# A decoder layer in split products: the bias table's exchange and the sums of the spatial weights multiplied with rounded and rest halves in place of plain f32 operands

## The chip, the cores and the metric

One NeuronCore of a Trainium2 chip runs the whole layer. The metric is the device time of one execution in microseconds (us); lower is better. TensorE multiplies, VectorE, ScalarE and GpSimd do the rest of the arithmetic, SyncE (SP) issues most of the transfers between DRAM and the on-chip memory. Each engine works through its own instructions in order and waits on semaphores of the others.

## The reference

A hybrid decoder layer over 2048 tokens of width 1024. What the change touches is the relative-position bias of the windowed attention, and the row sums of the spatial weights of the gated group.

```python
def chunked_spatial_gating(u, v, v_g, v_b, w_s, b_s):
    vg = v.reshape(b, s, A_GROUPS, A_GROUP_W)
    vg = (vg - mu) * lax.rsqrt(var + EPS)              # mu, var over the last axis
    vg = vg * v_g + v_b
    w = w_s * causal[None]                             # 4 x 128 x 128
    sv = jnp.einsum('gts,bnsgc->bntgc', w, vc) + b_s.T[None, None, :, :, None]
    return u * sv.reshape(b, s, A_WIDTH)

def sliding_window_attention(q, k, v, sinks, rel_bias):
    ...
    dist = qi + CHUNK - kj                             # 128 queries, 256 keys
    bias = rel_bias.astype(jnp.float32)[t5_causal_buckets(dist)]
    logits = jnp.where(valid, logits + bias, NEG)
    ...

def reference(...):
    h = rms_norm(x, pre_norm_g)
    a_u, a_v, sq, sk, sv, mq, z = jnp.split(h @ w_in, split_at, axis=-1)
    y_a = chunked_spatial_gating(gelu(a_u), gelu(a_v), ...)
    y_b = sliding_window_attention(sq, sk, sv, attn_sinks, rel_bias)
    y_c = memory_cross_attention(mq, *jnp.split(rms_norm(mem) @ w_mem_kv, 2))
    y = jnp.concatenate([y_a, y_b, y_c], axis=-1) * silu(z)
    return x + rms_norm(y @ w_out, post_norm_g)
```

## The kernel before, in words

The tokens are worked in four tiles (t = 0 to 3) of 512. For each tile the input projection is done unit by unit: four units of v, then sv, k, q_0, q_1, mq_0, mq_1, and the units of z and u, with the attention and gating work of the tile between them. The output projection follows. All numbers are f32, and large products are done in split form: an operand X is held as a rounded half (type float32r, made by a ScalarE copy) and the rest (X minus the rounded half, made by VectorE or GpSimd, also float32r). The helper `split(hi, lo, src)` makes both, and products add rounded x rounded, rounded x rest and rest x rounded in one PSUM bank. A few small products use plain f32 operands. TensorE works each plain f32 product as two recorded instructions.

TensorE's and SP's instructions run in the order of the code. VectorE, ScalarE and GpSimd are ordered by a scheduler when the program is built.

Weights come as units of 128x1024: `wraw` (raw, loaded by SP, three buffers), then `whl` (both halves), with the rest half on GpSimd for units 4 to 16 of the order and on VectorE else. In tile 0 there is also work that is done once:
- `first_stats` loads tile 0's rows of x (`xp`, four blocks in two buffers), ScalarE squares and sums them, VectorE (`rsa_x`) and GpSimd (`rsr_x`) make the row factors 1/rms. Everything that leaves PSUM in tile 0 is multiplied by these: v by ScalarE (`sc_v`), sv and k by VectorE (`sc_sv`, `sc_k`) with `bcs`, the factors spread along a row by a small product (`bc`).
- `load_constants` loads the spatial weights (`wsp`), their bias, and the sinks (`sink_bc`); GpSimd clears the triangle of `wsp`.
- `bias_vector` (in the first v unit) multiplies the bias table by a one-hot pattern into 4 x 383 numbers (`bv`), ScalarE copies them to `bvs` and issues their store to DRAM (`vec_d`). `bias_rows` (in the second v unit) is an SP load that reads this vector back with overlapping rows: 128 partitions, each with four runs of 256 numbers, every partition one number further on. `bias_turned` turns the order of the partitions by a product with an anti-diagonal matrix (`turn`), in two banks (`bt`), and ScalarE copies them to `bias`.
- `bias_constants` sums the columns of `wsp` by a product with a matrix of ones (`ad`), and VectorE makes `addend` of it. `bias_constants` and `bias_turned` stand on TensorE behind group q_0.

PSUM has two pools of four banks: `ps_mm` for groups and `ps_t` for the rest (among them g_sv, bc, g_k of tile 0, svt, ad, and both bt, which take the four banks in turn). A bank is free when VectorE or ScalarE has read the tile in it: `bt_1` stands where g_k stood, which `sc_k` reads.

`svt` are four transposes of `sc_sv`, in the middle of group g_q_0. The VectorE work of that stretch of tile 0 is the gelu and the normalization of v (`e_v`, `G_v`, `bn_stats`, `rsa_v`), the memory tokens (`hT<-mt`), `sc_sv` and `sc_k`. The order of SP's loads there is wraw_5, xp (third block), bias_rows, wraw_6, xp (fourth block), wraw_7, wsp, and so on.

Of the kernel before, what the change touches and what calls it, by code (L numbers as in the profile page):

```python
# [9 lines left out]
F32 = mybir.dt.float32  # L10
F32R = mybir.dt.float32r
# [38 lines left out]
def kernel(  # L50
# [33 lines left out]
    def f32(ap):  # L84
        return ap.bitcast(F32)
# [4 lines left out]
    def split(hi, lo, src, lo_engine=None, urgent=False):  # L90
        a = nc.scalar.copy(hi, src)  # L91
        b = (lo_engine or nc.vector).tensor_tensor(lo, src, f32(hi), ALU.subtract)  # L92
        if urgent:
            given["scalar"], given["vector"] = a, b
# [101 lines left out]
    ident = cp.tile([P, P], F32, name="ident")  # L196
    make_identity(nc, ident)

    turn = cp.tile([P, P], F32, name="turn")
    nc.gpsimd.memset(turn, 0.0)  # L200
    nc.gpsimd.affine_select(turn, turn, [[1, P]], ALU.not_equal, 1.0, base=1 - P, channel_multiplier=1)
    mhalf = tiny.tile([P, 4], F32, tag="mhalf", name="mhalf", bufs=1)
    nc.vector.memset(mhalf, -0.5)
    colt = tiny.tile([P, 24], F32, tag="colt", name="colt", bufs=1)
# [130 lines left out]
    wsp = cp.tile([P, 4, P], F32, name="wsp")  # L335
    bsp_t = sp.tile([P, 512], F32, tag="xk", name="bsp_t", bufs=2)
    sink_bc = tiny.tile([P, 4], F32, tag="sink_bc", name="sink_bc", bufs=1)
    ones = cp.tile([P, P], F32, name="ones")
    addend = cp.tile([P, 4, P], F32, name="addend")
    g_v = tiny.tile([P, 4], F32, tag="g_v", name="g_v", bufs=1)  # L340
    bias = cp.tile([P, 4, 256], F32, name="bias")
    vec_d = dram.tile([4, 383], F32, name="vec_d")

    def load_constants():
        nc.sync.dma_start(wsp, wspT)
        nc.sync.dma_start(bsp_t, bsp.broadcast_to([P, 512]))
        nc.sync.dma_start(sink_bc, sinks.broadcast_to([P, 4]))
        nc.vector.memset(ones, 1.0)
        nc.vector.tensor_scalar(g_v, colt[:, 16:20], 0.25, None, ALU.mult)

        nc.gpsimd.affine_select(wsp, wsp, [[0, 4], [1, P]], ALU.is_ge, 0.0, base=0, channel_multiplier=-1)

    def bias_constants():

        ad = ps_t.tile([P, 4, P], F32, tag="t", name="ad")
        nc.tensor.matmul(ad, ones, wsp, start=True, stop=True)
        for g in range(4):
            nc.vector.scalar_tensor_tensor(addend[:, g, :], ad[:, g, :], colt[:, 20 + g : 21 + g],
                                           bsp_t[:, g * P : (g + 1) * P], ALU.mult, ALU.add)
        nc.vector.tensor_scalar(addend, addend, 0.25, None, ALU.mult)  # L360

    def bias_vector():

        bv = ps_t.tile([4, 383], F32, tag="t", name="bv")
        nc.tensor.matmul(bv, rel_t, hot_t, start=True, stop=True)
        bvs = sp.tile([4, 383], F32, tag="e", name="bvs", bufs=3)
        nc.scalar.copy(bvs, bv)
        nc.scalar.dma_start(vec_d, bvs)

    def bias_rows():  # L370

        src = bass.AP(tensor=vec_d.tensor, offset=vec_d.offset, ap=[[1, P], [383, 4], [1, 256]])
        late["rows"] = sp.tile([P, 4, 256], F32, tag="O", name="bias_rows", bufs=1)
        nc.sync.dma_start(late["rows"], src)

    def bias_turned():

        for i in range(2):
            hs = slice(2 * i, 2 * i + 2)
            bt = ps_t.tile([P, 2, 256], F32, tag="t", name=f"bt_{i}")  # L380
            nc.tensor.matmul(bt, turn, late["rows"][:, hs, :], start=True, stop=True)
            nc.scalar.copy(bias[:, hs, :], bt)


# [309 lines left out]
    for t in range(NT):  # L694
# [14 lines left out]
        def run_jobs(first, last):  # L709

            for s in range(first, last):
                for job in jobs.pop(s, []):
                    job()
            tick[0] += 4
            flush_stores()
# [85 lines left out]
            nc.scalar.copy(KK[64:128, kv, :, P:], f32(KK[0:64, kv, :, P:]))  # L801

        run_jobs(-8, -4)

        def values(i):
            if i == (2 if t == 0 else 0):
# [450 lines left out]
```

## Time and profile before

| what | value |
|---|---|
| median of 3 runs | 765.74 us (765.73 to 765.94) |
| the profiled execution | 764.75 us, of it 762.9 us span of the engines |
| TensorE busy | 753.4 us, 99% of the span |
| VectorE, ScalarE, GpSimd busy | 565.9, 398.1, 113.0 us |
| DRAM traffic | 193.98 MB, mean 254 GB/s |

The span is the time between the first and the last instruction that the profiler saw, the execution's own time lies 1.85 us above it. A busy share is an average over the stages; a line of the timeline gives start, duration, engine, source line, operation and operands, and in brackets how long the engine sat idle before and what ended that.

### The profile page before, as it was taken

How to read it: one execution, taken by the hardware profiler on the slowest of the kernel's cores; microseconds unless marked ns; L12 is line 12 of the kernel's file. 1: busy time of each engine (PE TensorE's matmuls, PEld its weight loads, DVE VectorE, ACT ScalarE, POOL GpSimd, SP SyncE). 2: the span in 40 equal slices, each digit the busy share in tenths (PEclk: the TensorE clock that was granted, in tenths of full speed). 3: DMA queues.
4: the chain of work that ended last, by engine and by line, in shares of the span. 5: the costliest groups of instructions: out<-in, count | busy, mean ns of one | idle time of the engine just before them, and what ended most of it. 6: DMA issues, size and time to landing. Idle time of an engine off the chain costs nothing.

```text
span 762.9 us, 10628 instructions
## 1 busy us (share of the span) xinstructions
PE 753.4 (99%) x3764; PEld 636.3 (83%) x3764; DVE 565.9 (74%) x1072; ACT 398.1 (52%) x881; POOL 113.0 (15%) x122
## 2 busy tenths in 40 slices
PE   9999999999999999999999999999999999999995
PEld 7878988888888888888888888888888888888884
DVE  6396899996568888753889789748976325985787
ACT  7686775654735654455465454554444234443441
POOL 0556231000203200011132000201300000120002
PEclk9999999999999999999999999999999999999999
DMA  8847388977477898827779978664574699937618
GB/s 333 302 167 275 127 295 277 323 292 277 162 258 276 310 318 297 297 74 277 223 274 300 344 271 295 209 233 162 161 243 146 224 390 398 369 119 267 248 39 321
DMA packets 54134, 193.98 MB, mean 254 GB/s; under 512 B 5532, under 2 KB 6081, under 8 KB 44865
## 3 DMA queue, kind: packets, MB, share of 16 engines
q1 hardware_dynamic: 53552, 192.70, 71.4%
q8 instruction: 30, 0.49, 0.3%
q10 hardware_dynamic: 528, 0.59, 0.2%
q14 instruction: 24, 0.19, 0.1%
HBM read 140.84 MB, written 52.44 MB: 253 GB/s over the span
## 4 chain that ended last, share of the span: by engine, by line
PE 99%; DVE 0%; issue 0%; DVEq 0%; POOL 0%; ACT 0%; ACTq 0%; POOLq 0%
PE g_z L321 23%; PE g_u L321 12%; PE v L744 12%; PE g_q L321 6%; PE g_mq L321 6%; PE X_S L1108 6%; PE Y_S L1108 6%; PE Y L1108 6%; PE g_k L321 3%; PE X L1108 3%; PE g_sv L321 3%; PE o_c L572 2%; PE l_b L497 2%; PE l_c L548 2%; PE o_b L532 2%; PE sg L883 2%
## 5 line engine op out<-in xcount | busy, mean ns | idle before, releaser
L321 PE MATMUL g_z<-hT,whl 128*128 128x512 f32 x768 | 193.7, 396 | 0.0
L321 PEld LDWEIGHTS g_z<-hT,whl 128*128 128x128 f32 x768 | 138.4, 188 | 25.0
L321 PE MATMUL g_u<-hT,whl 128*128 128x512 f32 x384 | 97.7, 396 | 0.0
L744 PE MATMUL v<-whl,hT 128*128 128x512 f32 x384 | 88.5, 390 | 0.0
L744 PEld LDWEIGHTS v<-whl,hT 128*128 128x128 f32 x384 | 71.7, 188 | 15.8 <-issue 0.6
L321 PEld LDWEIGHTS g_u<-hT,whl 128*128 128x128 f32 x384 | 69.2, 188 | 12.7
L91 ACT CAST whl<-wraw 128x1024 fp32r<-128x1024 f32 (+1 forms) x43 | 44.2, 1027 | 35.2 <-DMA wraw<-in_wst 12.8
L191 POOL TENSOR_TENSOR rsr_v<-rsa_v,mhalf 128x4 f32<-128x4 f32 x16 | 16.8, 1055 | 213.0 <-DVE mv L769 193.2
L92 DVE TENSOR_TENSOR whl<-wraw,whl 128x1024 fp32r<-128x1024 f32 (+1 forms) x30 | 35.8, 1197 | 14.3 <-ACT whl L91 14.2
L321 PE MATMUL g_q<-hT,whl 128*128 128x512 f32 x192 | 45.9, 394 | 0.0
L321 PE MATMUL g_mq<-hT,whl 128*128 128x512 f32 x192 | 44.7, 389 | 0.0
L1108 PE MATMUL Y_S<-hT,yop_S 128*128 128x512 f32 x192 | 44.2, 389 | 0.0
L1108 PE MATMUL Y<-hT,yop 128*128 128x512 f32 x192 | 43.8, 389 | 0.0
L522 POOL TENSOR_SCALAR_AFFINE_SELECT pp_b<-po_b 128x512 fp32r<-128x512 f32 x30 | 20.6, 688 | 148.1 <-ACT po_b L91 148.1
L1108 PEld LDWEIGHTS Y<-hT,yop 128*128 128x128 f32 x192 | 36.0, 188 | 7.5
L1108 PEld LDWEIGHTS Y_S<-hT,yop_S 128*128 128x128 f32 x192 | 36.0, 188 | 7.5
L321 PEld LDWEIGHTS g_q<-hT,whl 128*128 128x128 f32 x192 | 35.8, 188 | 7.8 <-ACT SV L91 0.2
L321 PEld LDWEIGHTS g_mq<-hT,whl 128*128 128x128 f32 x192 | 35.8, 188 | 7.3
L1013 POOL TENSOR_TENSOR r<-a,mhalf 128x1 f32<-128x1 f32 x16 | 13.6, 853 | 190.9 <-DVE a L1011 184.8
L92 POOL TENSOR_TENSOR whl<-wraw,whl 128x1024 fp32r<-128x1024 f32 x13 | 31.6, 2439 | 30.7 <-ACT whl L91 30.2
L558 ACT ACTIVATE L_c<-l_c,nm_c 128x256 f32<-128x256 f32 x48 | 22.3, 471 | 24.5 <-DVE nm_c L553 24.3
L984 DVE TENSOR_TENSOR yop<-y,yop 128x1024 fp32r<-128x1024 f32 x12 | 14.6, 1219 | 24.0 <-ACT yop L975 24.0
(213 smaller groups left out, 1467.4 us busy)
## 6 DMA issues: line engine op xcount, KB each, us to landing
whl<-split_d SPq DMA_DIRECT2D x50, 1024.0 KB, 6.4
wraw<-in_wst SPq DMA_DIRECT2D x41, 512.0 KB, 5.9
split_d<-whl SPq DMA_DIRECT2D x18, 1024.0 KB, 8.0
hT<-wo_B SPq DMA_DIRECT2D x10, 1024.0 KB, 8.9
wo_T<-hT SPq DMA_DIRECT2D x8, 1024.0 KB, 8.5
xr<-in_x SPq DMA_DIRECT2D x16, 512.0 KB, 7.5
y<-yd SPq DMA_DIRECT2D x7, 1024.0 KB, 10.6
xj<-in_xT SPq DMA_DIRECT2D x12, 512.0 KB, 7.7
```

The costliest lines, as they stand in the source:

```text
L91: a = nc.scalar.copy(hi, src)
L92: b = (lo_engine or nc.vector).tensor_tensor(lo, src, f32(hi), ALU.subtract)
L191: nc.gpsimd.tensor_tensor(r, a, mhalf[:, :c], ALU.pow)
L321: nc.tensor.matmul(ps, w[:, wi, k * P : (k + 1) * P], hT[:, hi, k, :], start=(n == 0), stop=(n == 3 * KC - 1))
L497: nc.tensor.matmul(lg[:, e, :], S[kv][:, e, c * P : (c + 1) * P], KK[:, kv, s, c * P : c * P + 256], start=(s == 0), stop=(s == 1))
L522: nc.gpsimd.affine_select(prev[:, s], f32(own[:, s]), [[0, 4], [-1, P]], ALU.is_gt, 0.0, base=0, channel_multiplier=1)
L532: nc.tensor.matmul(o[:, kv, :], SV[:, c + w, kv].rearrange("p a b -> p (a b)"), pT, start=(n == 0), stop=(n == len(terms) - 1))
L548: nc.tensor.matmul(lg[:, e, :], S[:, h % 2, q0 : q0 + P], MK[:, h, s, :], start=(s == 0), stop=(s == 1))
L558: last = nc.scalar.activation(p[:, e, :], lg[:, e, :], AF.Exp, bias=nm[:, e : e + 1], scale=scale, accum_out=den[:, e : e + 1])
L572: nc.tensor.matmul(o, MV[:, j, h].rearrange("p a b -> p (a b)"), pT[:, s, j, :], start=(n == 0), stop=(n == 3))
L744: nc.tensor.matmul(vps[i], hT[:, hi, 2 * j + kk, i * P : (i + 1) * P], w[:, wi, kk * 512 : (kk + 1) * 512], start=(j == 0 and (hi, wi, kk) ...
L1108: nc.tensor.matmul(banks[m], a(s, k)[:, m * P : (m + 1) * P], w(v, k), start=first and n == 0, stop=n == 11, skip_group_check=not first)
```

## The change

`ones`, `turn`, `wsp`'s copy for the column sums and the bias vector become float32r operands. `ones` and `turn` hold numbers that need no rest. `bvs` gets two halves, both are stored to DRAM by one transfer (`vec_d` is [4, 2, 383] now) and read back by two SP loads in place of one, into buffers with the tags "O" and "S1" ("S1" held the second pair of x^T blocks before). `split_spatial`, behind the k unit of tile 0, splits `wsp`; the products of the gating (L883) keep the plain `wsp`. `ad` and the two `bt` become two float32r products each, rounded half and rest into the same bank.

```diff
-    turn = cp.tile([P, P], F32, name="turn")
-    nc.gpsimd.memset(turn, 0.0)
-    nc.gpsimd.affine_select(turn, turn, [[1, P]], ALU.not_equal, 1.0, base=1 - P, channel_multiplier=1)
+    turn = cp.tile([P, P], F32R, name="turn")
+    turn_0 = sp.tile([P, P], F32, tag="ZB", name="turn_0", bufs=2)
+    nc.gpsimd.memset(turn_0, 0.0)
+    nc.gpsimd.affine_select(turn, turn_0, [[1, P]], ALU.not_equal, 1.0, base=1 - P, channel_multiplier=1)
...
-    ones = cp.tile([P, P], F32, name="ones")
+    ones = cp.tile([P, P], F32R, name="ones")
...
-    vec_d = dram.tile([4, 383], F32, name="vec_d")
+    vec_d = dram.tile([4, 2, 383], F32, name="vec_d")
...
-        nc.vector.memset(ones, 1.0)
+        ones_1 = sp.tile([P, P], F32, tag="ZB", name="ones_1", bufs=2)
+        nc.vector.memset(ones_1, 1.0)
+        nc.vector.tensor_copy(ones, ones_1)
...
-        nc.tensor.matmul(ad, ones, wsp, start=True, stop=True)
+        for i, part in enumerate(late["wsp"]):
+            nc.tensor.matmul(ad, ones, part, start=i == 0, stop=i == 1)
...
-        bvs = sp.tile([4, 383], F32, tag="e", name="bvs", bufs=3)
-        nc.scalar.copy(bvs, bv)
-        nc.scalar.dma_start(vec_d, bvs)
+        bvs = sp.tile([4, 2, 383], F32R, tag="pT", name="bvs")
+        split(bvs[:, 0], bvs[:, 1], bv)
+        nc.scalar.dma_start(vec_d, f32(bvs))
...
-        src = bass.AP(tensor=vec_d.tensor, offset=vec_d.offset, ap=[[1, P], [383, 4], [1, 256]])
-        late["rows"] = sp.tile([P, 4, 256], F32, tag="O", name="bias_rows", bufs=1)
-        nc.sync.dma_start(late["rows"], src)
+        late["rows"] = [sp.tile([P, 4, 256], F32R, tag=tag, name=f"bias_rows_{tag}", bufs=1) for tag in ("O", "S1")]
+        for i, rows in enumerate(late["rows"]):
+            src = bass.AP(tensor=vec_d.tensor, offset=vec_d.offset + 383 * i, ap=[[1, P], [766, 4], [1, 256]])
+            nc.sync.dma_start(f32(rows), src)
+
+    def split_spatial():
+        late["wsp"] = [sp.tile([P, 4, P], F32R, tag="ZB", name=f"wsp_{i}", bufs=2) for i in range(2)]
+        split(*late["wsp"], wsp)
...
-            nc.tensor.matmul(bt, turn, late["rows"][:, hs, :], start=True, stop=True)
+            for n, rows in enumerate(late["rows"]):
+                nc.tensor.matmul(bt, turn, rows[:, hs, :], start=n == 0, stop=n == 1)
...
         run_jobs(-8, -4)
+        if t == 0:
+            split_spatial()
```

Three places show how instructions stand now. The first is SP's queue in the second v unit of tile 0, the kernel before and then the changed one (numbers at the end of a name count tiles and differ between the two).

```order
L138 DMA wraw_5_219<-in_wst 128x1024
L225 DMA xp_221<-in_x 128x1024
L374 DMA bias_rows<-vec_d 128x4x256
L138 DMA wraw_6_257<-in_wst 128x1024
L225 DMA xp_221<-in_x 128x1024
L138 DMA wraw_7_296<-in_wst 128x1024
```

```order
L138 DMA wraw_5_221<-in_wst 128x1024
L226 DMA xp_223<-in_x 128x1024
L379 DMA bias_rows_O<-vec_d 128x4x256
L379 DMA bias_rows_S_251<-vec_d 128x4x256
L138 DMA wraw_6_261<-in_wst 128x1024
L226 DMA xp_223<-in_x 128x1024
L138 DMA wraw_7_300<-in_wst 128x1024
```

A second load of rows stands ahead of wraw_6 and of the fourth block of x. The second place is VectorE in tile 0 between the row factors' first step (`rsa_x`) and `bcs`, before and then changed.

```order
L189 TENSOR_SCALAR rsa_x_261<-ss_156 128x4
L491 COPY Lc_b_0_743<-sink_bc 128x4
L790 TENSOR_SCALAR rstd_q<-rsr_x_263 128x4
L491 COPY Lc_b_1_817<-sink_bc 128x4
L583 SCALAR_TENSOR_TENSOR e_v_0_346<-e_v_0_346,sc_v_344 128x512
L583 SCALAR_TENSOR_TENSOR e_v_1_374<-e_v_1_374,sc_v_372 128x512
L407 SCALAR_TENSOR_TENSOR hT_92<-mt_328,colt,hT_92 128x256 x4
L583 SCALAR_TENSOR_TENSOR e_v_2_402<-e_v_2_402,sc_v_400 128x512
L277 COPY bcs_495<-bc_490 128x512
```

```order
L189 TENSOR_SCALAR rsa_x_265<-ss_157 128x4
L501 COPY Lc_b_0_756<-sink_bc 128x4
L800 TENSOR_SCALAR rstd_q<-rsr_x_267 128x4
L501 COPY Lc_b_1_830<-sink_bc 128x4
L92 TENSOR_TENSOR wsp_546<-wsp,wsp_545 128x512
L593 SCALAR_TENSOR_TENSOR e_v_0_352<-e_v_0_352,sc_v_350 128x512
L593 SCALAR_TENSOR_TENSOR e_v_1_380<-e_v_1_380,sc_v_378 128x512
L278 COPY bcs_501<-bc_496 128x512
L417 SCALAR_TENSOR_TENSOR hT_92<-mt_334,colt,hT_92 128x256 x4
```

The subtraction for `wsp`'s rest stands ahead of `e_v_0`, and `bcs` has moved ahead of the memory tokens' `hT`. (On ScalarE the copy for `wsp`'s rounded half stands behind the three `sc_v` and ahead of `e_v_0`; in the first v units VectorE has `bvs`' subtraction just ahead of `whl_3`, and ScalarE issues `vec_d` behind `whl_3`'s copy and ahead of `hT`, as before.) The third place is VectorE a little later, from `sc_sv` on, before and then changed.

```order
L330 TENSOR_TENSOR sc_sv_499<-g_sv_465,bcs_495 128x512
L769 BN_AGGR mv_0_353<-st_0_352 128x2 x2
L769 BN_AGGR mv_1_381<-st_1_380 128x2 x4
L189 TENSOR_SCALAR rsa_v_0_362<-mv_0_353 128x4
L189 TENSOR_SCALAR rsa_v_1_390<-mv_1_381 128x4
L583 SCALAR_TENSOR_TENSOR e_v_3_430<-e_v_3_430,sc_v_428 128x512
L330 TENSOR_TENSOR sc_k_531<-g_k_506,bcs_495 128x512
```

```order
L331 TENSOR_TENSOR sc_sv_505<-g_sv_471,bcs_501 128x512
L779 BN_AGGR mv_0_359<-st_0_358 128x2 x2
L779 BN_AGGR mv_1_387<-st_1_386 128x2 x4
L189 TENSOR_SCALAR rsa_v_0_368<-mv_0_359 128x4
L189 TENSOR_SCALAR rsa_v_1_396<-mv_1_387 128x4
L331 TENSOR_TENSOR sc_k_537<-g_k_512,bcs_501 128x512
L593 SCALAR_TENSOR_TENSOR e_v_3_436<-e_v_3_436,sc_v_434 128x512
```

`sc_k` has moved ahead of `e_v_3`. GpSimd's order in this stretch (`whl_6`, `rsr_x`, `wsp`, `whl_7`, `rsr_mem`, `whl_8`) is as before.

## Rows read from the trace of the kernel before

**Rows 1.** The page of the profile, its span, TensorE's line of part 1 (busy us, share of the span, instructions), the clock line of part 2 (tenths of full speed in 40 slices) and the first line of part 4 (the chain that ended last, by engine).

```profile
span 762.9 us, 10628 instructions
PE 753.4 (99%) x3764; PEld 636.3 (83%) x3764; DVE 565.9 (74%) x1072; ACT 398.1 (52%) x881; POOL 113.0 (15%) x122
...
PEclk9999999999999999999999999999999999999999
...
PE 99%; DVE 0%; issue 0%; DVEq 0%; POOL 0%; ACT 0%; ACTq 0%; POOLq 0%
```

**Rows 2.** The list of waits of TensorE over the whole span (us in total, times, longest).

```profile
PE warm L213 <- POOL ident masks.py:199: 1.5, 1, 1.5
```

**Rows 3.** The timeline of TensorE's products from 34 to 70 us (start us, us from first start to last end, engine, line, operation, out<-in, count).

```profile
34.52 5.72 PE L321 MATMUL g_k<-hT,whl 128*128 128x512 f32 x24
40.08 4.25 PE L321 MATMUL g_q<-hT,whl 128*128 128x512 f32 x18
44.16 0.60 PE L809 MATMUL svt<-ident,sc_sv 128*128 128x128 f32 x4
44.52 1.64 PE L321 MATMUL g_q<-hT,whl 128*128 128x512 f32 x6
45.99 1.02 PE L356 MATMUL ad<-wsp,ones 128*128 128x512 f32 x2
46.85 1.88 PE L381 MATMUL bt<-bias_rows,turn 128*128 128x512 f32 x4
...
54.03 11.04 PE L321 MATMUL g_mq<-hT,whl 128*128 128x512 f32 x48
64.91 4.24 PE L321 MATMUL g_z<-hT,whl 128*128 128x512 f32 x18
```

**Rows 4.** The timeline of TensorE's loads of weights from 43 to 49 us, same columns; in brackets the idle time before and what ended it.

```profile
43.93 0.58 PEld L809 LDWEIGHTS svt<-ident,sc_sv 128*128 128x128 f32 x4
...
47.50 0.40 PEld L381 LDWEIGHTS bt<-bias_rows,turn 128*128 128x128 f32 x2 [0.46 <-DVE sc_k L330]
...
48.56 5.20 PEld L321 LDWEIGHTS g_q<-hT,whl 128*128 128x128 f32 x23 [0.24 <-issue]
```

**Rows 5.** The timeline of ScalarE and of its DMA queue (ACTq) from 13 to 35 us.

```profile
13.87 1.04 ACT L91 CAST whl<-wraw 128x1024 fp32r<-128x1024 f32 x1
14.00 0.26 ACTq L368 DMA_DIRECT2D vec_d<-bvs  x1
14.90 1.34 ACT L288 ACTIVATE hT<-xj,colt 128x512 fp32r<-128x512 f32 x2
...
26.74 1.05 ACT L91 CAST whl<-wraw 128x1024 fp32r<-128x1024 f32 x1 [2.75 <-DMA wraw<-in_wst]
...
31.43 1.84 ACT L762 ACTIVATE sc_v<-v,rsr_x 128x512 f32<-128x512 f32 x3 [1.09 <-POOL rsr_x L191]
33.16 1.16 ACT L582 ACTIVATE e_v<-sc_v 128x512 f32<-128x512 f32 x2
```

**Rows 6.** The timeline of SP, which issues nearly all loads and stores, from 18 to 22 us (here the us are those that the issue takes).

```profile
18.64 0.33 SPq L225 DMA_DIRECT2D xp<-in_x  x1
19.06 1.86 SPq L374 DMA_DIRECT2D bias_rows<-vec_d  x1
21.02 0.46 SPq L138 DMA_DIRECT2D wraw<-in_wst  x1
```

**Rows 7.** The DMA view of three stretches: SP's queue from 18.5 to 21.5 us (packets, MB, share of the 16 engines' time), all packets and SP's queue from 21.5 to 24.5 us, and all packets from 25 to 28 us.

```profile
q1 hardware_dynamic: 183, 0.64, 64.2%
...
DMA packets 563, 0.66 MB, mean 220 GB/s; under 512 B 21, under 2 KB 529, under 8 KB 563
...
q1 hardware_dynamic: 563, 0.66, 92.6%
...
DMA packets 336, 1.21 MB, mean 404 GB/s; under 512 B 37, under 2 KB 37, under 8 KB 336
```

**Rows 8.** The timeline of GpSimd from 30 to 47 us.

```profile
30.38 1.02 POOL L191 TENSOR_TENSOR rsr_x<-rsa_x,mhalf 128x4 f32<-128x4 f32 x1
...
31.98 2.39 POOL L92 TENSOR_TENSOR whl<-wraw,whl 128x1024 fp32r<-128x1024 f32 x1
...
43.75 2.40 POOL L92 TENSOR_TENSOR whl<-wraw,whl 128x1024 fp32r<-128x1024 f32 x1
```

**Rows 9.** The timeline of VectorE from 13 to 48 us.

```profile
13.15 1.41 DVE L289 SCALAR_TENSOR_TENSOR hT<-xj,colt,hT 128x512 fp32r<-128x512 f32 x2
...
32.65 1.75 DVE L491 COPY Lc_b<-sink_bc 128x4 f32<-128x4 f32 x1 [2.35 <-DMA sink_bc<-in_sinks]
...
34.38 0.16 DVE L491 COPY Lc_b<-sink_bc 128x4 f32<-128x4 f32 x1
34.45 1.28 DVE L583 SCALAR_TENSOR_TENSOR e_v<-e_v,sc_v 128x512 f32<-128x512 f32 x2
...
43.01 0.65 DVE L330 TENSOR_TENSOR sc_sv<-g_sv,bcs 128x512 f32<-128x512 f32 x1
...
44.00 2.18 DVE L189 TENSOR_SCALAR rsa_v<-mv 128x4 f32<-128x4 f32 x1
46.17 0.68 DVE L583 SCALAR_TENSOR_TENSOR e_v<-e_v,sc_v 128x512 f32<-128x512 f32 x1
46.77 0.68 DVE L330 TENSOR_TENSOR sc_k<-g_k,bcs 128x512 f32<-128x512 f32 x1
```

## The prediction

> **What bounds the kernel now.** I read the page first. TensorE is busy for 753.4 of 762.9 us, the chain that ended last is TensorE for 99%, and the granted clock stands at full speed in every slice [rows 1]. The list of who TensorE waited for has one entry, 1.5 us at the very start [rows 2]. So the kernel is a line of products without gaps. A microsecond taken out of that line is a microsecond of the result, and so is every wait put into it, because nothing later has slack to swallow it.
>
> Then I read the timeline of the stretch that the change touches, 13 to 50 us. On TensorE [rows 3] the eye should follow svt, ad and bt in the middle of the groups g_q. A rounded 128x512 product takes 10.88 / 48 = 0.227 us (g_mq, 54.03 to 64.91). A plain one is two records of 0.43: ad from 45.99 to 46.85. The loads of weights [rows 4] show what the modelled ends hide: bt's second product had to wait for sc_k on VectorE until 47.50 (sc_k frees the PSUM bank of g_k, which bt_1 takes), and group g_q_1 runs at its pace from 48.56 on. The other place is svt: VectorE ended sc_sv at 43.01 + 0.65 = 43.66, and TensorE came for it at 43.93, so there is only 0.27 us of slack [rows 4, 9].
>
> What feeds these two places? Going back: sc_sv is the end of a VectorE run without a gap that begins at 34.45 (e_v_0) and lasts 9.21 us. It begins when one tiny copy (Lc_b<-sink_bc) lets go at 32.65 + 1.75 = 34.40, a copy that takes 1.75 us, where the next of its kind takes 0.16, because GpSimd's whl_7 runs until 31.98 + 2.39 = 34.37 [rows 8, 9]. GpSimd got there after rsr_x, which needs the fourth block of x (xp), and that block lands behind wraw_6. ScalarE shows it: it waits 2.75 us for wraw_6 until 26.74 [rows 5]. And wraw_6 stands on SP's queue just behind bias_rows, whose issue alone takes 1.86 us [rows 6]. **So the load of bias_rows stands at the head of a tight chain: bias_rows, wraw_6, xp, rsr_x, whl_7, VectorE's run, sc_sv, TensorE.**
>
> **What the change does to it, part by part.**
>
> *The products.* ad and two bt: 3 x 0.86 = 2.58 us go, six rounded ones of 0.227 = 1.36 come. At most 1.2 us is won, if TensorE never waits there.
>
> *The rest of the bias vector.* VectorE computes bvs' second half. It is free at 13.15 + 1.41 = 14.56 [rows 9]; a 128x512 subtraction from PSUM takes 0.65 (sc_sv), so 383 columns take 0.49 and end at 15.05, before whl_3's rounded half is there (13.87 + 1.04 = 14.91, so VectorE loses 0.1). But ScalarE's DMA issue of vec_d now waits for it, 15.05 in place of 14.00, and with its 0.26 holds the next instruction, hT, to 15.3 instead of 14.90 [rows 5]. ScalarE has no gap between there and the xp squares, so SP's next load, xp at 18.64, which waits for these squares, slips by 0.4. Where vec_d's later write would still be on its way when bias_rows is issued (19.5 in place of 19.06), that adds up to 0.5; no row tells when it landed, only that it was before 19.06.
>
> *The second load of rows.* This is the part that costs. SP issues a second 512 KB load of 1 KB pieces: 1.9 us more before wraw_6. So by the issue alone wraw_6 is late by 0.4 + 1.9 = 2.3. By the DMA engines it is more: from 21.5 to 24.5 they moved 508 packets of about 1 KB (0.52 MB) and 0.14 MB of others at a busy share of 92.6%; the others take 0.14 / 0.404 = 0.35 us, the 1 KB packets therefore 0.926 x 3.0 - 0.35 = 2.4 us [rows 7]. Then wraw_6 is late by 0.4 + 2.4 = 2.8. I take 2.6 and call it d. The lower bound is 1.7, if 512 KB took only 0.52 / 0.404 = 1.3 us as loads of large packets do; the upper is 3.3 with vec_d's 0.5. The page "DMA: Bandwidth & Descriptors" of the Trainium skill (section Specifications) speaks for that lower bound: line rate from 512 B on. By that rule d is 1.7; the trace's 1 KB packets at about 220 GB/s do not bear it out.
>
> *Down the chain with d = 2.6.* rsr_x ends at 31.40 + 2.6 = 34.0 (TensorE reaches bc before that and waits 0.3 to 0.5, which is not added: it waits longer at svt anyway). whl_7 ends at 34.37 + 2.6 = 36.97, and the held copy with it.
>
> *The split of the spatial weights.* Its rounded half is a ScalarE CAST of 512 columns, taken as one of the three sc_v, (33.16 - 31.43) / 3 = 0.58 [rows 5], put behind them: 33.16 + 2.6 + 0.58 = 36.34, in time for VectorE's subtraction at 37.05. That subtraction (0.60, as e_v from start to start: 1.28 for two of 0.68) [rows 9] is new in front of e_v_0, so the run starts at 34.45 + 2.6 + 0.6 = 37.65 and ends 9.21 later: sc_sv at 46.86. ScalarE is 3.2 late there too, but its results (e_v's tanh) are still wanted later than they come. Without that cover the CAST would cost 0.58 more.
>
> *TensorE.* svt starts 0.25 after sc_sv: 47.1 in place of 44.16. From svt to ad it is 1.83, so ad at 48.93, bt_0 at 49.4, bt_1 ready at 49.85. Now sc_k: VectorE's rsa_v before it was held by GpSimd's whl_8 (44.00 to 46.18 against 43.75 + 2.40 = 46.15) [rows 8, 9]. whl_8 follows a small GpSimd operation (rsr_mem) whose input comes out of the same VectorE run, some 3.0 later, so it runs to 49.2; sc_k now stands ahead of e_v_3 and gains that 0.6: 49.25 to 49.95. bt_1 starts at 50.2 and its two products end at 50.65. Before, that point was 48.6. **The sum: 2.0 us later**, with the 1.2 of the shorter products already in it. If rsa_v slips in ahead of whl_8, bt_1 goes at 49.85 and the delay is 1.75. Small sets (memsets, the CAST of ones, turn through a second tile) run before 2 us on idle engines, and cost nothing; later groups find their weights halves ready several us ahead (g_mq at 56 wants whl_8, done at 49.2), so nothing is added there.
>
> The profiled execution has a span of 762.9 and a time of 764.75, and would have 764.9 and 766.75. The median of the runs is 765.74, 1.0 above it, so the forecast is 765.74 + 2.0 = **767.7 us**.
>
> **Rivals.** Differences up to 0.2% (1.53 us) are about what a measurement of this kernel can tell from none; by the sum above that bound is crossed at d = 2.1.
> - *Not slower: the second load is hidden.* If wraw_6's lateness does not reach xp and rsr_x (d near 0), svt waits 0.25, sc_k is ready before bt_1 and most of the products' gain stays: 1.0 off, 764.7. For it: between 18.5 and 21.5 the DMA engines are busy for only 64.2% [rows 7]. Against it: xp is on its way then, wraw_6 stands behind the rows on one queue, and ScalarE waits visibly for it. It decides below a d of about 0.6, where delay and gain cancel. Chance 0.12.
> - *Partly hidden*: 1 KB packets at the rate of the large ones, or ScalarE not held: d 1.7, a delay of 1.1, 766.8; between d = 0.6 and 2.1 the time is 765.7 to 767.3. Chance 0.23.
> - *The clock.* TensorE would wait about 2.6 us at svt, longer than any wait of the trace (1.5). If the granted clock fell to its lower level, 1.2 GHz, each following 128x512 product would cost 0.227 more: 12 of them 2.7, 770.4. No row shows a fall; chance 0.05. The Trainium skill's "TensorE: Matmul & The Clock Gate" (Part 1) lets an idle engine fall to that level; no run here shows it so far.
> - *The pairs don't pay*: rounded products with these operands could cost as much as plain ones; then 1.2 more. The kernel's own groups of such products speak against it; it is inside the range, with no chance of its own.
>
> **Chances.** The forecast's case (d 2.1 to 3.4, 767.3 to 768.7) has 0.57. With the clock's 0.05 slower has 0.62; the two hidden cases lie within 0.2% for almost all of their 0.35, and 0.03 is left for faster, which would need more than the whole gain of the products. The range 765.4 to 769.2 leaves out half of the fully hidden case and the clock's.
>
> **What would show it.** Right: bias_rows twice on SP with 1.9 us each, wraw_6 issued 2.3 later (23.3); ScalarE's wait for wraw_6 ending near 29.3; rsr_x ending near 34.0; the copy of sink_bc letting go near 37.0; wsp's subtraction right behind it; TensorE waiting 2 to 3 us for sc_sv at svt and shortly for sc_k at bt_1; g_q_1 at pace from 50.65; all later groups shifted by the same 2.0. Wrong: xp and rsr_x within 1 us of their old places, svt without a wait, or a shift that grows or shrinks after 55 us.

## The result and the profile after

The changed kernel takes **769.24 us** (median of six runs, 768.02 to 769.92) against 765.79 us for the kernel before in the same comparison (six runs, 765.73 to 766.00). The medians lie 3.45 us apart; the ratio over all runs is 1.0043, with a 95% interval of 1.0033 to 1.0053. The direction was forecast, the size was not: 767.7 was predicted, 2.0 us more, and the median lies 0.04 us above the upper end of the range.

The profiled execution of after took 769.92 us with a span of 767.9. Against the profiled execution of before that is 5.2 us and not 3.45, because the one lies 0.7 above its median and the other 1.0 below. So sizes below are read as differences of places in the two traces, and only medians are called the price of an edit.

The page, against [rows 1], its span, TensorE's line and the clock:

```profile
span 767.9 us, 10634 instructions
PE 753.4 (98%) x3764; PEld 636.2 (83%) x3764; DVE 569.3 (74%) x1075; ACT 397.6 (52%) x882; POOL 112.4 (15%) x122
...
PEclk9999999999999999999999999999999999999998
```

TensorE is as busy as before and the clock as high. Of the 5.0 us of span 4.20 are TensorE standing still: its last group of products starts at 748.09 in place of 743.89. The other 0.8 lie behind that group, and such a rest belongs to the single execution: in the run e8 below the last group starts 0.01 early and the span is still 1.2 longer than before's. Where TensorE stands still, the list of waits of its weight loads tells for the first 120 us (us in total, times, longest):

```profile
PEld svt L821 <- DVE sc_sv L331: 2.4, 1, 2.4
PEld mvt L462 <- ACT mvs L455: 1.5, 1, 1.5
...
PEld o_b L542 <- POOL po_b L534: 0.9, 1, 0.9
...
PEld bt L391 <- DVE sc_k L331: 0.4, 1, 0.4
PEld bc L275 <- POOL rsr_x L191: 0.4, 1, 0.4
```

svt, bt and bc are places that the prediction named. mvt and o_b, whose waits end at 94.73 and 114.54 us, are not. There are two losses, then, and the prediction has only the first.

**The first loss, 20 to 54 us.** ScalarE and its DMA queue, against [rows 5]:

```profile
15.06 0.26 ACTq L372 DMA_DIRECT2D vec_d<-bvs  x1
15.37 1.34 ACT L289 ACTIVATE hT<-xj,colt 128x512 fp32r<-128x512 f32 x2 [0.44 <-DVE bvs L92]
...
28.96 1.05 ACT L91 CAST whl<-wraw 128x1024 fp32r<-128x1024 f32 x1 [4.45 <-DMA wraw<-in_wst]
...
35.38 0.63 ACT L91 CAST wsp<-wsp 128x512 fp32r<-128x512 f32 x1
```

ScalarE is held to 15.37 and waits for wraw_6 until 28.96, 2.22 later than before. SP, against [rows 6]:

```profile
19.41 1.09 SPq L379 DMA_DIRECT2D bias_rows_O<-vec_d  x1
20.55 0.50 SPq L379 DMA_DIRECT2D bias_rows_S<-vec_d  x1
21.14 0.53 SPq L138 DMA_DIRECT2D wraw<-in_wst  x1
```

Two issues take 1.09 + 0.50 where one took 1.86, so wraw_6 is issued at 21.14, only 0.12 later than before. Its lateness comes from behind the issue, from the transfers. All packets from 21.5 to 24.5 us, against the second line of [rows 7]:

```profile
DMA packets 395, 0.41 MB, mean 138 GB/s; under 512 B 15, under 2 KB 387, under 8 KB 395
```

138 GB/s, where the rows of before ran at 220. GpSimd and VectorE, against [rows 8, 9]:

```profile
34.20 2.40 POOL L92 TENSOR_TENSOR whl<-wraw,whl 128x1024 fp32r<-128x1024 f32 x1
```

```profile
33.08 0.17 DVE L501 COPY Lc_b<-sink_bc 128x4 f32<-128x4 f32 x1 [0.56 <-DMA sink_bc<-in_sinks]
...
36.04 1.10 DVE L92 TENSOR_TENSOR wsp<-wsp,wsp 128x512 fp32r<-128x512 f32 x1 [1.72 <-ACT wsp L91]
37.07 1.28 DVE L593 SCALAR_TENSOR_TENSOR e_v<-e_v,sc_v 128x512 f32<-128x512 f32 x2
...
45.62 0.65 DVE L331 TENSOR_TENSOR sc_sv<-g_sv,bcs 128x512 f32<-128x512 f32 x1
...
48.51 0.68 DVE L331 TENSOR_TENSOR sc_k<-g_k,bcs 128x512 f32<-128x512 f32 x1
```

The small copies of sink_bc now come before whl_7 (34.20) and are free in 0.17; in before one was held for 1.75. In its place VectorE waits 1.72 for the CAST of wsp, and the run e_v to sc_sv starts at 37.07 in place of 34.45. (The subtraction of wsp itself takes 1.10 and not the 0.69 that it takes in e11, where no subtraction of GpSimd runs beside it; here whl_7 runs until 36.60.) TensorE's weight loads, against [rows 4]:

```profile
46.32 0.42 PEld L821 LDWEIGHTS svt<-ident,sc_sv 128*128 128x128 f32 x4 [2.36 <-DVE sc_sv L331]
...
49.25 0.19 PEld L391 LDWEIGHTS bt<-bias_rows_O,turn 128*128 128x128 f32 x1 [0.39 <-DVE sc_k L331]
...
49.59 5.46 PEld L322 LDWEIGHTS g_q<-hT,whl 128*128 128x128 f32 x24
```

g_mq starts at 55.32, 1.29 later than in [rows 3].

**The second loss, 72 to 116 us.** VectorE, ScalarE and GpSimd between 54 and 92 us fall from about 1.3 to 4.8 us behind. The changed program has another order there: the splits of q (S_q_0, S_q_1, S_mq_0) stand ahead of the normalization of v (nb, vhat), and on GpSimd units 15 and 30 ahead of rsr_v_2 and rsr_v_3. Then two VectorE instructions are held (KK are the keys, Lc_b the logits of the windowed attention). GpSimd's units 32 and 18, and VectorE:

```profile
74.44 2.39 POOL L92 TENSOR_TENSOR whl<-wraw,whl 128x1024 fp32r<-128x1024 f32 x1 [0.69 <-ACT whl L91]
...
83.75 2.81 POOL L92 TENSOR_TENSOR whl<-wraw,whl 128x1024 fp32r<-128x1024 f32 x1 [0.34 <-POOL whl L92]
```

```profile
74.11 0.88 DVE L510 SCALAR_TENSOR_TENSOR Lc_b<-l_b,rstd_q,bias 128x256 f32<-128x256 f32 x2
74.90 2.21 DVE L794 CAST KK<-KK 128x512 fp32r<-128x512 f32 x1
...
84.22 2.61 DVE L514 TENSOR_TENSOR Lc_b<-L_b 128x256 f32<-128x256 f32 x1
```

The same places in the kernel before (VectorE):

```profile
69.92 0.88 DVE L500 SCALAR_TENSOR_TENSOR Lc_b<-l_b,rstd_q,bias 128x256 f32<-128x256 f32 x2
70.71 0.81 DVE L784 CAST KK<-KK 128x512 fp32r<-128x512 f32 x1
...
78.89 1.93 DVE L504 TENSOR_TENSOR Lc_b<-L_b 128x256 f32<-128x256 f32 x1
...
92.78 0.68 DVE L505 TENSOR_REDUCE nm_b<-Lc_b 128x4 f32<-128x516 f32 x1
```

Lc_b of the first window starts at 74.11 in place of 69.92. The CAST of KK takes 2.21 and ends 0.3 behind unit 32's subtraction, the addition to Lc_b takes 2.61 and ends 0.3 behind unit 18's. A hold need not cost anything: in before one addition takes 1.93 beside a unit that runs from 78.14 to 80.54, and TensorE doesn't wait. There ScalarE's mvs (the copy that TensorE transposes at mvt) ends at 89.61, 2.37 ahead of its use at 91.98. In the changed kernel it ends at 94.67, 5.06 later, which is more than this slack and TensorE's own lateness of 1.29 together. So TensorE waits:

```profile
94.73 0.20 PEld L462 LDWEIGHTS mvt<-ident,mvs 128*128 128x128 f32 x2 [1.53 <-ACT mvs L455]
...
114.54 0.19 PEld L542 LDWEIGHTS o_b<-po_b,SV 128*128 128x128 f32 x1 [0.92 <-POOL po_b L534]
```

After that TensorE is 4.2 us late, and stays so to its last group. These places in before (mvs, mvt, and the third start of l_c, the logits of the memory attention), and then mvs and l_c in the changed kernel:

```profile
89.24 0.37 ACT L445 COPY mvs<-gm 128x256 f32<-128x256 f32 x1
...
91.98 0.38 PE L452 MATMUL mvt<-ident,mvs 128*128 128x128 f32 x2
...
115.38 0.72 PE L548 MATMUL l_c<-MK,S_mq 128*128 128x256 f32 x4
```

```profile
94.30 0.37 ACT L455 COPY mvs<-gm 128x256 f32<-128x256 f32 x1
...
119.58 0.71 PE L558 MATMUL l_c<-MK,S_mq 128*128 128x256 f32 x4
```

### The profile page after: what moved, and what is told of

It is laid out like the page before. It is cut to its first block, busy times and chain, and to the rows that moved or that the text cites. A ratio compares the mean times of both kernels' runs of the same rounds, so it can differ in the third digit from the quotient of the medians.

```text
span 767.9 us, 10634 instructions
## 1 busy us (share of the span) xinstructions
PE 753.4 (98%) x3764; PEld 636.2 (83%) x3764; DVE 569.3 (74%) x1075; ACT 397.6 (52%) x882; POOL 112.4 (15%) x122
## 5 line engine op out<-in xcount | busy, mean ns | idle before, releaser
L517 ACT ACTIVATE Lc_b<-Lc_b,nm_b 128x129 f32<-128x129 f32 x64 | 25.0, 393 | 20.7 <-DVE nm_b L515 20.4
```

What stands on the lines that cost most here:

```text
L517: last = nc.scalar.activation(Lc[:, h, : P + 1], Lc[:, h, : P + 1], AF.Exp, bias=nm[:, h : h + 1], accum_out=den[:, h : h + 1])
```

## The experiments

Three theories of the second loss were set against each other. **A**: the new order of splits and units makes VectorE late, and that is the whole of it. **B**: any chain that is late by 1.3 us grows later, whatever the order. **C** (formed after the first four runs): GpSimd's subtractions hold VectorE for 2 us at a bad moment, and the order only sets the moment. Of the first loss, A in its first texts also says that it is the second load's time on the queue.

This table has what the traces show: when ScalarE begins to split wraw_6, and by how much TensorE is late against before at four places (svt, g_mq, mvt and l_c: 44.16, 54.03, 91.98 and 115.38 us in before). The profile is one execution, the median is of 5 to 12; "run" is the profiled execution's own time. The ratio is taken over all runs, so it need not be that of the medians. The 0.30 of e4 and the 0.80 of e9 are there from bv at 11 us on, with the first loads, and belong to no edit.

| kernel | wraw_6 | svt | g_mq | mvt | l_c | run | median | ratio (95%) |
|---|---|---|---|---|---|---|---|---|
| before | 26.74 | 0 | 0 | 0 | 0 | 764.75 | 766.08 (765.79 beside e9 to e12) | 1 |
| after, e5 | 29.49 | 2.70 | 1.80 | 3.32 | 4.79 | 770.66 | 769.63 | 1.0050 (1.0038, 1.0062) |
| e1 order as before | 29.07 | 2.28 | 2.68 | 2.69 | 2.69 | 767.98 | 766.40 | 1.0013 (1.0001, 1.0025) |
| e8 units on VectorE | 27.71 | 0.90 | -0.03 | -0.02 | -0.02 | 766.05 | 766.59 | 1.0009 (1.0000, 1.0018) |
| e9 before, units on VectorE | 26.47 | 0.80 | 0.80 | 0.80 | 0.80 | 766.78 | 766.15 | 1.0001 (0.9993, 1.0010) |
| e2 weights' sums only | 26.79 | 0.20 | 0.29 | 1.34 | 2.80 | 768.55 | 765.54 | 0.9999 (0.9990, 1.0007) |
| e3 bias exchange only | 28.49 | 1.09 | 0.41 | 0.41 | 0.41 | 766.49 | 766.42 | 1.0004 (0.9996, 1.0013) |
| e4 before, two loads | 26.90 | 0.30 | 0.30 | 0.30 | 0.30 | 765.64 | 766.36 | 1.0005 (0.9997, 1.0014) |
| e6 second load late | 27.59 | 0.78 | 0.47 | 0.48 | 0.47 | 766.70 | 766.47 | 1.0007 (0.9997, 1.0017) |
| e7 both loads late | 26.17 | 3.71 | 5.19 | 5.19 | 5.17 | 770.79 | 768.54 | 1.0037 (1.0026, 1.0049) |
| e10 = e6 + e8 | 29.11 | 2.31 | 1.99 | 2.00 | 2.00 | 767.70 | 766.55 | 1.0009 (0.9999, 1.0020) |
| e11 = e10, wsp later | 26.61 | 0.55 | 1.28 | 1.28 | 1.28 | 766.89 | 769.19 | 1.0042 (1.0026, 1.0058) |
| e12 = e8, wsp later | 30.02 | 3.28 | 2.09 | 2.09 | 2.83 | 768.76 | 768.76 | 1.0043 (1.0031, 1.0055) |

### The changed kernel again (e5)

No edit.

> The changed kernel itself, timed beside the others on this chip, since the first four runs left single executions of one kernel up to 4 us apart. If the 3.4 us belong to the kernel: 768.5 to 769.5 us here too, TensorE 1.3 us late at 54 us and about 4 us late at 116 us in this profile too. If a large part of them belongs to how the transfers at 20 to 28 us happened to run: 766 to 768 us, with another split between 54 and 116 us.

769.63 us, ratio 1.0050, just above the 768.5 to 769.5 expected. The 3.5 us belong to the kernel. Its trace has the same waits (svt 2.3, mvt 1.6, o_b 0.9) and the same held instructions (2.22 and 2.62), all 0.5 us later than in the first profile: wraw_6 came 0.5 later and everything behind it followed.

### The order put back (e1)

```diff
...
-            with behind_given() if (u, t) in LATE else ExitStack():
+            after_vhat = {11: 2, 12: 3}.get(i)
+            with behind_given() if (u, t) in LATE else behind(("rsr", "v0_3"), ("vhat", 0, after_vhat)) if after_vhat else ExitStack():
...
+            v, n = {"q0_0": ((0, 1), (1, 2)), "q0_1": ((2, 3), (3, 3)), "mq0_0": ((3, 3), (3, 3))}.get(tag, ((None, None), (None, None)))
+            with behind(("vhat", 0, v[e]), ("nb", 0, n[e]), *more) if v[e] is not None else ExitStack():
-            nc.scalar.copy(S[0:64, e, :], src)
-            nc.vector.tensor_tensor(S[64:128, e, :], src, f32(S[0:64, e, :]), ALU.subtract)
+                nc.scalar.copy(S[0:64, e, :], src)
+                norm["S", tag, e] = nc.vector.tensor_tensor(S[64:128, e, :], src, f32(S[0:64, e, :]), ALU.subtract)
...
```

> The changed kernel, with the splits of q and of the first memory query held behind the normalization of v in tile 0 and weight units 15 and 30 held behind rsr_v_3, as they stood in the kernel before (order of issue only; the work is the same). Theory A (the second loss, 1.3 us at 54 us growing to 4.2 us at 116 us, comes from the new order of the splits and units on VectorE, ScalarE and GpSimd): TensorE is about 1.3 us late at 54 us and still about 1.3 us late at 116 us, time about 767.1 us. Theory B (the second loss is only what a late chain costs, whatever the order): late by 1.3 us at 54 us and by about 4 us at 116 us, time about 769 us.

766.40 us, 3.2 less than the changed kernel and 0.7 less than A's 767.1. TensorE is 2.7 us late at 54 us, more than in the changed kernel, and still exactly that late at 115 us. Its weight loads at mvt show no wait:

```profile
94.56 0.25 PEld L470 LDWEIGHTS mvt<-ident,mvs 128*128 128x128 f32 x2
```

B falls: a longer lateness did not grow. Against the expectation the first part was larger, and the table by stage shows why (us, busy times by engine, then granted clock, DMA share, GB/s):

```profile
48.00:54.00 6.00, 6.00 (x23) 4.80 (x22) 5.87 (x11) 4.62 (x7) 5.89 (x5) 0.79 0.25 90
```

The clock granted between 48 and 54 us is 0.79: after the wait of 2.29 us at svt it stood at its lower level, 1.2 GHz, from 47.1 to 50.5 us, and TensorE went from 2.28 late (svt) to 3.37 (ad). That is the prediction's rival, seen here in one execution.

### GpSimd's units moved (e8, and e9 as its control)

```diff
-                split(w[:, 0, c], w[:, 1, c], raw[:, c], nc.gpsimd if 4 <= i <= 16 else nc.vector)
+                split(w[:, 0, c], w[:, 1, c], raw[:, c], nc.gpsimd if 4 <= i <= 13 else nc.vector)
```

> The changed kernel with the rests of weight units 32, 33 and 18 taken on VectorE (three subtractions of about 1.2 us) and not on GpSimd. Theory C (the second loss arises when a unit's subtraction on GpSimd holds a VectorE copy for 2 us or more, at 75 and 84 us): no VectorE instruction between 72 and 92 us takes over 1.3 us, VectorE's lag at 92 us shrinks from 5 to 4 us or less, time about 768 us. Theory A (the order of the splits of q is the whole of it): VectorE's lag stays or grows by up to 3.7 us, 769 us or more.

> The kernel before, in plain f32, with the rests of weight units 32, 33 and 18 taken on VectorE and not on GpSimd: the control of the same move in the changed kernel. Theory C (the holds by these units cost time only where VectorE is already late): TensorE waits for nothing there in the kernel before, so the time stays within 0.4 us of it. If the move is a gain to any kernel: 1.5 us or more below it.

e8: 766.59 us, 3.0 less than the changed kernel, though VectorE got 3.6 us more work and kept the order of the splits. Its VectorE, at the places shown above:

```profile
72.85 0.88 DVE L510 SCALAR_TENSOR_TENSOR Lc_b<-l_b,rstd_q,bias 128x256 f32<-128x256 f32 x2
73.65 0.41 DVE L794 CAST KK<-KK 128x512 fp32r<-128x512 f32 x1
...
75.18 1.21 DVE L92 TENSOR_TENSOR whl<-wraw,whl 128x1024 fp32r<-128x1024 f32 x1
...
81.79 0.42 DVE L514 TENSOR_TENSOR Lc_b<-L_b 128x256 f32<-128x256 f32 x1
...
92.74 0.68 DVE L515 TENSOR_REDUCE nm_b<-Lc_b 128x4 f32<-128x516 f32 x1
```

Lc_b starts at 72.85, 2.9 late against before with TensorE on time (-0.03): that is the order's lateness, still there. (It has holds of its own in it: rsa_v of the last two blocks of v takes 1.90 and 1.25 here, 1.89 and 1.25 in the changed kernel, beside units 15 and 30 on GpSimd, and 0.17 each in before. What they are worth alone no run tells.) But the CAST takes 0.41 and not 2.21, the addition 0.42 and not 2.61, and by nm_b of the third window VectorE is at 92.74, where it was in before (92.78). From 50 to 125 us TensorE waits for nothing. So A falls as the whole cause: the order's 2.9 us are absorbed where no unit holds VectorE. My own number for C was too careful (768): I had not counted that the new work lies mostly in VectorE's idle time. e9 gives the control: the same move in the kernel before changes nothing (ratio 1.0001), so e8 didn't gain from a better kernel but from the missing holds.

### The parts alone (e2, e3)

e2 keeps the exchange in plain f32, e3 the sums.

```diff
-        bvs = sp.tile([4, 2, 383], F32R, tag="pT", name="bvs")
-        split(bvs[:, 0], bvs[:, 1], bv)
+        bvs = sp.tile([4, 383], F32, tag="e", name="bvs", bufs=3)
+        nc.scalar.copy(bvs, bv)
...
```

```diff
-        for i, part in enumerate(late["wsp"]):
-            nc.tensor.matmul(ad, ones, part, start=i == 0, stop=i == 1)
+        nc.tensor.matmul(ad, ones, wsp, start=True, stop=True)
...
-        if t == 0:
-            split_spatial()
```

> Only the sums of the spatial weights in halves; the bias table's exchange stays in plain f32, one load of rows. Theory A with its first loss put on the second load of rows: wraw_6 is split at the time of before (26.7 us), the rest subtraction of wsp adds up to 0.6 us on VectorE and the shorter sums give back up to 0.5, so TensorE is within 0.5 us of before at 54 us; GpSimd's order is that of before, so nothing more comes, time 765.5 to 766.4 us. Rival (the split of wsp is what makes VectorE late): TensorE late by 1 us or more at 54 us, time 767 us or more.

> Only the bias table's exchange in halves, with its second load of rows; the sums of the spatial weights stay in plain f32. Theory A: wraw_6 is split 2.2 us late as in the changed kernel, TensorE is 0.7 to 1.3 us late at 54 us, and as units 15 and 30 stand as in the changed kernel the second loss of about 2.9 us comes too: 768.5 to 769.5 us. Theory B: about the same. Rival (the split of wsp is the cause): within 0.5 us of before.

Neither part costs anything that can be measured (0.9999 and 1.0004), and 3.5 us are not the sum of the two. e3 missed A's 768.5: it has the rows' delay (wraw_6 at 28.49) and the changed order of the splits, but GpSimd's unit 30 stands behind rsr_v_3 again (I had expected it ahead), and there is no second loss. e2 shows that GpSimd's new order is not needed for one either. Its median is 765.54, but its profiled execution, the longest of twelve, lost 2.5 us between 54 and 115 us with GpSimd's order as in before. GpSimd's units 33 and 18 and VectorE in that execution:

```profile
79.72 2.67 POOL L92 TENSOR_TENSOR whl<-wraw,whl 128x1024 fp32r<-128x1024 f32 x1 [3.41 <-ACT whl L91]
83.11 2.41 POOL L92 TENSOR_TENSOR whl<-wraw,whl 128x1024 fp32r<-128x1024 f32 x1 [0.72 <-ACT whl L91]
```

```profile
80.21 2.73 DVE L600 SCALAR_TENSOR_TENSOR Z_z<-Z_z,sc_z 128x512 f32<-128x512 f32 x1
...
83.20 2.36 DVE L498 COPY Lc_b<-sink_bc 128x4 f32<-128x4 f32 x1
```

Two other instructions are held, one of them a copy of four columns for 2.36 us. So, as this one execution shows it, C needs only that VectorE meets a unit at a bad moment, however it came there.

e3 and the changed kernel together also price the split of wsp, with one execution of each: sc_sv starts 11.39 us behind the end of rsr_x without it and 12.00 with it. The difference is 0.6 us. (In before it is 11.61.)

### Where the rows are loaded (e4, e6, e7)

e4 is the kernel before with the rows loaded twice, the second copy unused, and e1's holds:

```diff
...
         nc.sync.dma_start(late["rows"], src)
+        late["rows2"] = sp.tile([P, 4, 256], F32, tag="S1", name="bias_rows2", bufs=1)
+        nc.sync.dma_start(late["rows2"], src)
...
```

> The kernel before, in plain f32, with the rows of the bias table loaded twice (the second copy is used by nothing) and with the holds of the first of these runs. Theory A: the second load makes wraw_6 2.2 us late and TensorE about 2 us late at 54 us, with nothing of shorter products to give back and nothing more later: 767.6 to 768.0 us. Theory B: the lateness grows as in the changed kernel, 769.5 us or more. If the second load is free: 765.8 us.

766.36 us (1.0005). A's 767.6 to 768.0 is missed. In the profiled execution, one of the two shortest of twelve, both loads together held wraw_6 up by 0.16. From 21.5 to 24.5 us they ran at more than twice the rate of the changed kernel:

```profile
DMA packets 911, 0.93 MB, mean 310 GB/s; under 512 B 20, under 2 KB 905, under 8 KB 911
```

e6 and e7 issue the second load, or both, behind the loads of the constants and of the memory (in e6 each call of bias_rows issues one load, in e7 the call in the second v unit is gone):

```diff
             if t == 0 and j == 3:
                 load_constants()
                 prep = prep_memory()
                 next(prep)
+                bias_rows()
...
```

> The changed kernel with the second load of rows issued after wraw_7, the constants and the first memory loads, not ahead of wraw_6. Theory A (the first loss is the second load's time on the queue ahead of wraw_6): wraw_6 is split at 26.5 to 27.3 us as in the kernel before, TensorE at most 0.7 us late at 54 us, time 765.5 to 766.5 us. If what is late comes from the split of wsp or from the write of vec_d: TensorE about 1.3 us late at 54 us, 767 us or more.

> The changed kernel with both loads of rows issued there. Theory A: wraw_6 lands 2 to 4 us earlier than in the kernel before (24 to 25 us), rsr_x and all behind it by as much until another wait ends last; the rows land before 40 us, ahead of their use at 47 us. TensorE 1 to 2 us early at 54 us, time 764 to 765 us. If the path does not begin at wraw_6: 766 us.

e6's time came out as expected (766.47), but its trace doesn't carry the reason: with one load ahead of it wraw_6 is at 27.59, outside the 26.5 to 27.3 expected, and in e10, which has the same loads, at 29.11. By number of loads ahead, wraw_6 was split at 26.17 (none, e7), 26.5 to 26.8 (one, in before's layout: before, e2, e9), 26.61, 27.59 and 29.11 (one, in the layout with both halves), 26.90 (two, before's layout), and 27.71 to 30.02 with a mean of 29.0 (two, both halves, six executions). In either layout wraw_6 is later with more rows ahead, but what a load costs varies by 2 us between executions, and one load is no fixed 2.2. Why the layout with both halves is slower, with one to six executions of each, stays open.

e7 is a plain miss: wraw_6 is 0.57 early, the time 2.5 us above before. The subtraction of wsp, now beside whl_7, is held, the first rsa_v, which now stands ahead of sc_sv, is held by whl_8, and sc_sv ends 4.2 us later than in before. VectorE, TensorE's weight loads, and the table by stage from 48 to 54 us:

```profile
34.19 2.48 DVE L92 TENSOR_TENSOR wsp<-wsp,wsp 128x512 fp32r<-128x512 f32 x1 [2.73 <-ACT wsp L91]
...
45.05 1.80 DVE L189 TENSOR_SCALAR rsa_v<-mv 128x4 f32<-128x4 f32 x1
```

```profile
47.87 0.71 PEld L820 LDWEIGHTS svt<-ident,sc_sv 128*128 128x128 f32 x4 [3.91 <-DVE sc_sv L331]
```

```profile
48.00:54.00 6.00, 6.00 (x17) 4.85 (x18) 5.46 (x11) 3.03 (x7) 4.43 (x3) 0.53 0.68 205
```

The granted clock is 0.53 there: it went to 1.2 GHz at 46.8 us, while TensorE waited 3.91 us, and came back at 53.6. The lateness went from 3.7 (svt) to 5.2 (g_mq), though the shorter products lie in this stretch.

### Both repairs, and wsp later (e10, e11, e12)

e10 joins e6 and e8. e11 and e12 put wsp's split behind the first products of e_v_0 and e_v_1:

```diff
-            split_spatial()
+            with tc.issue_after(late["first", "v0_1"].ins):
+                split_spatial()
```

> The changed kernel with the second load of rows issued behind wraw_7 and the first memory loads, and the rests of units 32, 33 and 18 on VectorE. Theories A and C together (first loss from the load, second from the holds): both losses gone but for 0.4 us of the split of wsp, the shorter products give 0.9 us back by 54 us, time 765.2 to 766.0 us, at most 0.8 us below the kernel before. If the two edits do not add up: 766.5 us.

> As the run before it, and the rest of wsp taken on VectorE behind the first products of e_v_0 and e_v_1, not ahead of them. If the split of wsp is on the path: e_v_0 starts right behind rsr_x, 0.4 us or more earlier against it than in the changed kernel, time 764.6 to 765.6 us. If it is hidden: the same as the run before it.

> The changed kernel with both loads of rows where the change puts them, units 32, 33 and 18 on VectorE, and the rest of wsp behind e_v_0 and e_v_1. What it lacks against the run before it is the later second load alone: if that load costs 1 to 2 us on the path, 766.0 to 767.0 us; if it is mostly hidden, within 0.3 us of the run before it.

e10 is 766.55: the two repairs do not add up. In the traces e6 and e8 each lack the second loss already, and e10's own execution has a first loss of 1.99, since wraw_6 is late there although the second load stands behind it. With wsp later the kernel is slower by 2.2 to 2.6 us, against both expectations. Between e12 (768.76) and e11 (769.19) the place of the second load makes no difference that can be measured. The profiled execution of e11 shows one reason for the loss. GpSimd takes units 8 and 9 in a row, and e_v_3's product, which now stands ahead of sc_k, is held:

```profile
43.31 4.75 POOL L92 TENSOR_TENSOR whl<-wraw,whl 128x1024 fp32r<-128x1024 f32 x2
```

```profile
45.72 2.88 DVE L595 SCALAR_TENSOR_TENSOR e_v<-e_v,sc_v 128x512 f32<-128x512 f32 x1
48.53 0.68 DVE L331 TENSOR_TENSOR sc_k<-g_k,bcs 128x512 f32<-128x512 f32 x1
```

TensorE waits 2.1 us for sc_k at bt. That execution was the shortest of its seven, 2.3 below the median; what the others lose beside this no trace shows. e12's profiled execution, at its median, has none of this hold at sc_k, but the latest wraw_6 of all (30.02): TensorE is 2.09 late at g_mq and 2.83 at l_c. No version is faster than the kernel before by more than its measurement can tell.

## Why the prediction was right in direction and short in size

- **SP's issue, 1.9 us for the second load: wrong.** Both issues together took 1.59, less than the one before, and wraw_6 was issued at 21.14, not 23.3. An issue's duration was not the load's price: the first load of rows took 0.38 to 1.86 us to issue in these runs, and in e2, where it took 0.39, wraw_6's own issue behind it took 1.49. What decides it no run shows.
- **d = 2.6 by the DMA engines: nearly right in this kernel.** 2.22 and 2.75 in the two executions, but by a slow stretch (138 GB/s) and not by a fixed price per packet: e4 moved the same bytes at 310 GB/s and lost 0.16. The lower bound of 1.7 from large packets' rate was no lower bound. The Trainium skill's "DMA: Bandwidth & Descriptors" (Specifications) gives line rate from 512 B on. The trace is nearer to that in e4 than in the changed kernel: e4's 310 GB/s with 1 KB packets are closer to the 404 of large ones [rows 7] than the changed kernel's 138, so the packet's size alone doesn't decide it.
- **The held copy of sink_bc to 37.0: wrong, and in place of it a wait.** The copy slipped in ahead of whl_7, which gave 0.22 back by sc_sv (e3 against before), and the split of wsp took 0.61 (computed: 0.60), so sc_sv came 2.61 late where rsr_x was 2.22 late. The forecast had 3.20 there, with its d of 2.6. Of the 2.61 the slack at svt took 0.44, where the forecast had 0.26: svt came 2.17 late, not 2.94.
- **TensorE behind svt: right.** Predicted to regain 0.94 of the delay, it regained 0.88 by g_mq. The wait at svt was 2.36 (2 to 3), the one at bt_1 0.39, rsa_v was held by whl_8 for 1.92, and sc_k ended at 49.19 (49.95). The sum was +2.0 and is +1.29 at g_mq.
- **"All later groups shifted by the same 2.0": the step that failed.** Nothing was added, I wrote, since the weights of later groups are ready early. I looked at weights alone, and not at the order in which VectorE, ScalarE and GpSimd take up their work between 46 and 92 us, though the change had reordered it. There TensorE's lateness grew by 2.9 us, from 1.29 to 4.20. The order made VectorE 2.9 us late (e8), two units of GpSimd held it by 1.8 and 2.2 more, and without these two holds 3.0 of the 3.5 us are gone (e8). The last sign on the prediction's own list, a shift that grows after 55 us, is what the trace shows.
- **The rivals.** The clock's fall was real, in e1 after a wait of 2.29 and in e7 during one of 3.91, but not in either trace of the changed kernel (1.00 in every stage to 120 us), whose waits were 2.36 and 2.3; what decides between these no run tells. The rival's twelve slow products, 2.7 us, came from no row: e1's fall made TensorE 1.1 us later. The Trainium skill's "TensorE: Matmul & The Clock Gate" (Part 1), an idle engine falls to the lower level, is borne out by e7. "Partly hidden" describes what is left when the second loss is gone: by their ratios e1, e6, e8 and e10 are 0.5 to 1.0 us above before, and of their intervals only e1's lies wholly above 1.

So where the forecast had one loss of 2.0, the profile has a first loss of 1.3 and a second one that I had put at zero. By the runs without the second loss, the first alone is worth 0.5 to 1.0 us in the time, half of the forecast or less, and would hardly be told from none. That the forecast has the right direction and is off by no more than about 1.5 us is owed in part to a loss that it didn't contain: that is luck.

## What to carry to other kernels

When an edit lets a scheduler reorder the engines beside the bottleneck, their order has to be read as far as the program keeps the new order, not only to where the edit's own waits end. Look on VectorE for instructions several times as long as their like, and on GpSimd for what ends with them; in the kernel before a slack of 2.4 us hid one such hold, and behind a late order two were too many. A price taken from one execution's transfers needs a second look before it is called a bound.

## What the runs showed of the hardware

- **GpSimd's subtraction holds some VectorE instructions to its end.** CAST of KK 2.21 against 0.41, addition to Lc_b 2.61 against 0.42 (e8), a copy of 128x4 2.36 (e2) against 0.16, all with operands in SBUF. Products that read PSUM were not: sc_sv took 0.67 at 43.31 in e11, inside GpSimd's 43.31 to 48.06, and two of L_b took 1.40 at 81.46 in the changed kernel, inside 81.00 to 83.42. The Trainium skill's page "SBUF — State Buffer" (Who interferes with whom) states it: a VectorE instruction with two inputs in SBUF, or in a mode that uses both ports, is blocked wholly while a GpSimd instruction that reads SBUF has the shared pair. The traces agree, the small copy included.
- **Loads in 1 KB packets ran at 133 (e6) to 310 GB/s (e4)** in the same stretch of kernels that differ little, and wraw_6 behind the same loads came between 26.61 (e11) and 29.11 us (e10).
- **The granted clock fell to 1.2 GHz** from 47.1 to 50.5 us in e1, after TensorE had waited 2.29 us, and from 46.8 to 53.6 us in e7, where it waited 3.91 us. TensorE became 1.1 us (e1, svt to ad) and 1.5 us (e7, svt to g_mq) later there, the second with the gain of the shorter products in it.
